# Hybrid decoder layer on one core: the output projection's two middle column blocks as seven block products each, with operand sums made under the first block and results sent by way of DRAM

## The chip, the cores and the metric

One Trainium2 chip, one of its eight cores, one launch of one program. The metric is the device time of that core in microseconds (us), smaller is better. Times are compared with the median of several runs of the kernel before; the profile is one further execution, with its own time.

## What is computed

One layer of a decoder for 512 tokens of width 2048, everything in float32. Cut to what matters here:

```python
def token_mixer(h, w_in, ..., w_o, lambda_init):
    proj = h @ w_in
    ...
    o_a = (rmsnorm(gla_chunked(...), gla_norm) * gate).reshape(B, S, GLA_V)        # 512 x 1024
    o_b = (rmsnorm(diff_attention(...), diff_norm) * (1.0 - lambda_init)).reshape(B, S, DIFF_V)   # 512 x 1024
    o = jnp.concatenate([o_a, o_b], axis=-1)
    return o @ w_o                                                                 # 512x2048 @ 2048x2048

def reference(x, ...):
    h = rmsnorm(x, attn_pre_norm[l])
    m = token_mixer(h, ...)
    x = x + rmsnorm(m, attn_post_norm[l])
    h = rmsnorm(x, ffn_pre_norm[l])
    f = conv_ffn(h, w_ffn_in[l], conv_w[l], conv_b[l], w_ffn_out[l])
    x = x + rmsnorm(f, ffn_post_norm[l])
    return x
```

The case is about `o @ w_o`, the output projection, and about what stands on either side of it.

## The kernel before, in words

**Products.** A float32 operand is split into a high part and a low part of a narrower float32 form (`act(hi, raw, AF.Copy)` on ACT, L138 or L151, then `tt(lo, raw, hi, subtract)` on DVE, L139 or L152). A product is three matmuls: high by high, high by low, low by high. The activations of all 512 tokens lie split in `ah` and `al`, 4 tiles of 128 tokens by 16 slots of 128 columns. Weights come from DRAM in granules of 512 KB into one of four buffers `raw` and are split into one of three places of `ring`. So a granule can be split when its bytes have landed and the granule three before it has been used.

**A plain column block.** `proj_n` (L198) makes 512 columns for all tokens: 8 granules, each with 24 matmuls (4 token tiles, 2 slots, 3 products) that stream 512 columns of weights past a stationary 128x128 tile of activations. That is 192 matmuls. Four PSUM banks collect the four token tiles. `step()` after each granule advances side work (`fill`, a list of generators) at a rate set in `pace`.

**A unit of seven block products.** `InUnit` (L784) makes a 512-column block with tokens and the 2048 rows of the contraction each cut in two and the columns cut in two: seven products of sums of blocks instead of eight products of blocks. Its parts are called `x0`, `z0`, `y0`, `z1`, `x1`, `y1`, `y2`. Each part has 2 granules and 48 matmuls that stream 256 columns; a unit has 336. The operand sums of the tokens' side stand in `sums`: `a11`, `a12`, `a22` are blocks of `ah`/`al` themselves, `s5` is a21-a22, `s2` is s5-a11, `s3` is s2+a12, and `s7` is a11-a21, which is written over the block a21 of `ah`/`al`. The sums of the weights' side are made by DMAs on POOL's queue that add a second block from DRAM onto a granule already loaded (`more`, L806), and by one addition on DVE (L855). All input projections but the first three blocks, and both FFN products, already run this way.

**The output projection before.** The inputs are `o_a` (slots 8 to 15, written by `turn_gate`, L927) and `o_b` (slots 0 to 7, written by `place_diff`, L934, from `dstd` in DRAM). Rows of `w_o` are taken in the order of slots 8 to 15, then 0 to 7. Three column blocks run as `proj_n` (L1039), each with `evac_m` (L1033): an ACT square with a running sum, and a DVE product with the norm's gain into `m`, in SBUF. The fourth block runs in `to_ffn` (L1044), which follows an order written out by hand on PE, ACT, DVE and POOL. For token tile t it does the block's products, `evac`, then `residual` (L1063, which needs `xr`, the layer's input, and all 2048 columns of `m`), `square`, `scale` (needs the gain row `g2`), and `turn` (PE transposes and splits into `ah`/`al` for the FFN). The four tiles are staggered so that one tile's products stand over another's norm.

**What sets the order.** Outside such hand-ordered regions a planner orders each engine's instructions, by a timeline of its own: of the instructions that it holds to be ready it takes the one that comes first in the program. Each engine then runs its list in order. `keep_in_program_order` pins an instruction behind the one written just before it on its engine. The pool `wo` (tiles `m`, `g1`, `g2`, `xr`, and spare places `xhi`/`xlo` for split weights) takes over the bytes of the mixer's pools; a tile of it waits for the last user of its own bytes.

Of the kernel before, what the change touches and what calls it, by code (L numbers as in the profile page):

```python
# [17 lines left out]
P = 128  # L18
D = 2048
S = 512  # L20
NT = S // P
KT = D // P
# [3 lines left out]
DH, DQK, DDV = 4, 128, 256  # L26
# [9 lines left out]
def hybrid_layer(ctx: ExitStack, tc: tile.TileContext, x, attn_pre_norm, w_in, w_alpha_up, b_alpha,  # L36
# [10 lines left out]
    def dma(o, i):  # L47
        return nc.sync.dma_start(out=o, in_=i)
# [3 lines left out]
    act = nc.scalar.activation  # L52
    tt = nc.vector.tensor_tensor
# [6 lines left out]
    few = ctx.enter_context(tc.tile_pool(name="few", bufs=1, side="right"))  # L60
# [19 lines left out]
    fill = []  # L80
# [3 lines left out]
    def step(n=None):  # L84
        pace[1] += pace[0]
        while pace[1] >= 1.0:
            pace[1] -= 1.0
            while fill:
                try:
                    next(fill[0])  # L90
                    break
                except StopIteration:
                    fill.pop(0)

    def drain():
        while fill:
            for _ in fill.pop(0):
                pass
# [51 lines left out]
    def split(hi, lo, src):  # L150
        act(hi, src, AF.Copy)  # L151
        tt(lo, src, hi.bitcast(F32), ALU.subtract)  # L152
# [10 lines left out]
    def bcast_row(tile_ap, row):  # L163
        dma(tile_ap, row.partition_broadcast(P))
# [178 lines left out]
    HK = KT // 2  # L343
# [16 lines left out]
    def part_of(i, j):  # L360
        return [v[:, 2 * i:2 * i + 2, HK * j:HK * (j + 1), :] for v in (ah, al)]
# [419 lines left out]
    def two(v):  # L781
        return v.rearrange("p (n x) -> p n x", n=2)

    class InUnit:  # L784
# [8 lines left out]
        def block(self, i, j, g):  # L793
            return w_in3[:, HK * i + 4 * g:HK * i + 4 * g + 4, self.cols[j]:self.cols[j] + 256]
# [136 lines left out]
            turn_block(0, j, i, u)  # L931
            turn_block(1, j, i, kept_u.pop((j, i)))

    def place_diff(i):  # L934
        for h in range(DH):
            u = qk_tile("dt")
            dma(two(u), dstd[h][:, :, 256 * i:256 * (i + 1)])
            hi, lo = (v[:, 2 * i:2 * i + 2, 2 * h:2 * h + 2, :].rearrange("p t n c -> p n t c") for v in (ah, al))
            u = u.rearrange("p (n t c) -> p n t c", n=2, t=2)
            tc.keep_in_program_order(act(hi, u, AF.Copy))  # L940
            tc.keep_in_program_order(tt(lo, u, hi.bitcast(F32), ALU.subtract))

    def gv_out(t, b):
        u = block_tile("gv")
# [77 lines left out]

    x1d = [dram.tile([P, D], F32, name=f"x1d{t}") for t in range(NT)]
# [3 lines left out]
    g1 = wp.tile([P, D], F32, name="g1")  # L1027
    g2 = wp.tile([P, D], F32, name="g2")
    bcast_row(g1, attn_post_norm[0])
    bcast_row(g2, ffn_pre_norm[0])  # L1030
    ssm = [few.tile([P, 4], F32, name=f"ssm{t}") for t in range(NT)]

    def evac_m(c, t, b):  # L1033
        sl = slice(512 * c, 512 * (c + 1))
        act(m[t][:, sl], b, AF.Square, accum_out=ssm[t][:, c:c + 1])
        tt(m[t][:, sl], b, g1[:, sl], ALU.mult)

    slots = [(s + HK) % KT for s in range(KT)]
    for c in range(3):  # L1039
        proj_n(w_o3, 512 * c, lambda t, b, c=c: evac_m(c, t, b), slots)  # L1040

    def to_ffn():  # L1044
        banks = [bank(psm) for _ in range(NT)]
        w, wa, wb, xr, rs = {}, {}, {}, {}, {}

        def weights(g):
            w[g] = granule(w_o3[:, 2 * g:2 * g + 2, 1536:2048], 2, spare=wp if g > 3 else None)

        def prods(t, *gs):
            for g in gs:
                mm_n(banks, t, g, w[g], slots)

        def evac(t):
            xr[t] = wp.tile([P, D], F32, name="xr", tag="xr", bufs=2)
            dma(xr[t], x2[t * P:(t + 1) * P, :])
            evac_m(3, t, banks[t])
            ss = small.tile([P, 1], F32, name="ss", tag="ss")
            nc.vector.reduce_sum(ss, ssm[t], axis=AX.X)  # L1060
            rs[t] = rsqrt_mean(ss, D)

        def residual(t):  # L1063
            stt(m[t], m[t], rs[t], xr[t], ALU.mult, ALU.add)
            dma(x1d[t], m[t])

        def square(t):
            ss = small.tile([P, 1], F32, name="ss", tag="ss")
            act(xr[t], m[t], AF.Square, accum_out=ss)
            rs[t] = rsqrt_mean(ss, D)  # L1070

        def scale(t):
            for i in range(4):
                sl = slice(512 * i, 512 * (i + 1))
                stt(xr[t][:, sl], m[t][:, sl], rs[t], g2[:, sl], ALU.mult, ALU.mult)
# [407 lines left out]
        nxt.z0()  # L1483

    acc = []
    ssf = [few.tile([P, 4], F32, name=f"ssf{t}") for t in range(NT)]
# [317 lines left out]
```

## Time and profile before

| what | value |
|---|---|
| median of 3 runs | 2066.2 us (2065.96 to 2068.63) |
| the profiled execution's own time | 2066.0 us |
| its span in the trace | 2064.3 us |
| granted TensorE clock | 0.999 of full speed |
| TensorE busy | 99% of the span |
| VectorE, ScalarE, GpSimd busy | 73%, 49%, 14% |
| output projection, plain blocks 1 to 3 | 594.6 to 726.5 us of the span |
| the hand-ordered region after them | from 726.5 us on |

The profile has a page of totals and views of the trace: a timeline of single instructions by engine, windows (busy time of each engine in a stretch), groups of instructions by line, and the DMA issues with their time to landing. PE is TensorE's matmuls, PEld its weight loads, DVE VectorE, ACT ScalarE, POOL GpSimd, SP the engine that issues most DMAs. A matmul's row has a start and a modelled length; consecutive matmuls overlap in the pipeline, so what one costs is the distance between two starts, not its length.

### The profile page before, as it was taken

Reading aid. Unit: us, or ns where it says so; the run is one execution under the profiler, and the core shown is the slowest. Engines: PE = TensorE matmul, PEld = TensorE weight load, DVE = VectorE, ACT = ScalarE, POOL = GpSimd, SP = SyncE. Lnnn points to the kernel's source line nnn. Section 1 sums busy time; section 2 is a strip of 40 time slices with the busy share of each in tenths; the row PEclk is TensorE's granted clock in tenths of the full one; section 3 lists DMA queues with packets and bytes.
Section 4 is the critical chain, followed back from the end, with each engine's and each line's share of the span. In section 5 each row is a group of like instructions: output and inputs, shape, how many; then the busy total and the mean of one; then the engine's idle time right before and its main releaser. Section 6 shows DMA issues by size and latency. Waiting matters only on the chain.

```text
span 2064.3 us, 35589 instructions
## 1 busy us (share of the span) xinstructions
PE 2049.0 (99%) x14453; PEld 1897.7 (92%) x14453; DVE 1510.0 (73%) x1802; ACT 1002.9 (49%) x1309; POOL 292.3 (14%) x303
## 2 busy tenths in 40 slices
PE   9999999999999999999999999999999999999998
PEld 7799999999998889899999999999999988888886
DVE  7957777666762265977777777777777888988977
ACT  5544444555552243454554454555455654444443
POOL 2012223222200000011011111111111111111100
PEclk9999999999999999999999999999999999999999
DMA  5488887888874354368577577567668796776663
GB/s 206 141 183 182 200 189 176 194 180 209 190 233 148 101 179 159 102 129 193 144 163 188 136 165 188 136 167 179 146 157 199 207 260 181 193 199 170 169 178 122
DMA packets 281611, 358.09 MB, mean 173 GB/s; under 512 B 14865, under 2 KB 223173, under 8 KB 279526
## 3 DMA queue, kind: packets, MB, share of 16 engines
q1 hardware_dynamic: 192292, 259.33, 37.4%
q0 software_dynamic: 84800, 94.38, 30.1%
q8 instruction: 113, 1.85, 0.4%
q10 hardware_dynamic: 4354, 2.10, 0.4%
q14 instruction: 52, 0.43, 0.1%
HBM read 311.20 MB, written 44.56 MB: 172 GB/s over the span
## 4 chain that ended last, share of the span: by engine, by line
PE 72%; issue 23%; POOL 2%; DVE 2%; ACT 1%; DMA 1%; POOLq 0%; DVEq 0%; ACTq 0%
PE bank L1441 6%; PE bank L1439 6%; PE bank L1440 6%; PE bank L1339 4%; PE bank L1337 4%; PE bank L1338 4%; PE bank L192 3%; PE bank L194 3%; PE bank L193 3%; PE bank L830 3%; PE bank L834 3%; PE bank L836 3%; PE bank L835 3%; PE bank L832 3%; PE bank L831 3%
## 5 line engine op out<-in xcount | busy, mean ns | idle before, releaser
L138 ACT ACTIVATE ring<-raw 128x1024 fp32r<-128x1024 f32 x315 | 333.9, 1061 | 496.5 <-PE bank L1338 109.5
L139 DVE TENSOR_TENSOR ring<-raw,ring 128x1024 fp32r<-128x1024 f32 x315 | 383.4, 1223 | 258.2 <-ACT ring L138 257.5
L138 ACT ACTIVATE ring<-rt 128x1024 fp32r<-128x1024 f32 x221 | 234.3, 1062 | 249.1 <-PE bank L1338 145.4
L1339 PE MATMUL bank<-ah,ring 128*128 128x256 f32 x1280 | 353.5, 276 | 0.8 <-DVE ring L139 0.8
L1337 PE MATMUL bank<-ah,ring 128*128 128x256 f32 x1280 | 353.5, 276 | 0.0
L1338 PE MATMUL bank<-al,ring 128*128 128x256 f32 x1280 | 353.4, 276 | 0.0
L139 DVE TENSOR_TENSOR ring<-rt,ring 128x1024 fp32r<-128x1024 f32 x221 | 270.0, 1223 | 89.8 <-ACT ring L138 86.9
L1339 PEld LDWEIGHTS bank<-ah,ring 128*128 128x128 f32 x1280 | 240.3, 188 | 1.0 <-DVE ring L139 1.0
L1337 PEld LDWEIGHTS bank<-ah,ring 128*128 128x128 f32 x1280 | 240.3, 188 | 0.1
L1338 PEld LDWEIGHTS bank<-al,ring 128*128 128x128 f32 x1280 | 240.3, 188 | 0.1
L1440 PE MATMUL bank<-ring,ah 128*128 128x512 f32 x424 | 165.0, 389 | 0.0
L1441 PE MATMUL bank<-ring,al 128*128 128x512 f32 x424 | 165.0, 389 | 0.0
L1439 PE MATMUL bank<-ring,ah 128*128 128x512 f32 x424 | 152.1, 389 | 0.0
L193 PE MATMUL bank<-ring,ah 128*128 128x512 f32 x280 | 109.3, 390 | 0.1
L192 PE MATMUL bank<-ring,ah 128*128 128x512 f32 x280 | 108.9, 393 | 0.1
L194 PE MATMUL bank<-ring,al 128*128 128x512 f32 x280 | 108.1, 390 | 0.1
L1285 POOL DMA_DIRECT2D raw<-in_w_ffn_in_dram x40 | 51.2, 1309 | 397.7 <-DVE ring L139 397.7
L1285 POOL DMA_DIRECT2D rt<-in_w_ffn_in_dram x40 | 51.0, 1288 | 324.6 <-DVE ring L139 312.9
L1441 PEld LDWEIGHTS bank<-ring,al 128*128 128x128 f32 x424 | 79.6, 188 | 16.6
L1440 PEld LDWEIGHTS bank<-ring,ah 128*128 128x128 f32 x424 | 79.6, 188 | 16.6
L1439 PEld LDWEIGHTS bank<-ring,ah 128*128 128x128 f32 x424 | 79.6, 188 | 16.5
L834 PE MATMUL bank<-ring,ah 128*128 128x256 f32 x320 | 91.8, 287 | 0.0
(393 smaller groups left out, 5671.4 us busy)
## 6 DMA issues: line engine op xcount, KB each, us to landing
raw<-in_w_ffn_in_dram SPq DMA_DIRECT2D x96, 512.0 KB, 5.0
raw<-in_w_in_dram SPq DMA_DIRECT2D x56, 512.0 KB, 4.3
raw<-in_w_ffn_out_dram SPq DMA_DIRECT2D x46, 512.0 KB, 5.8
raw<-in_w_in_dram POOLq DMA_DIRECT2D x40, 512.0 KB, 6.9
rt<-in_w_ffn_in_dram SPq DMA_DIRECT2D x40, 512.0 KB, 5.7
rt<-in_w_ffn_in_dram POOLq DMA_DIRECT2D x40, 512.0 KB, 6.2
raw<-in_w_ffn_in_dram POOLq DMA_DIRECT2D x40, 512.0 KB, 7.2
raw<-in_w_o_dram SPq DMA_DIRECT2D x32, 512.0 KB, 4.0
```

Source lines behind the costliest of these rows:

```text
L138: act(hi, raw, AF.Copy)
L139: tt(lo, raw, hi.bitcast(F32), ALU.subtract)
L192: mm(banks[t], ah[:, t, s, :], w[0][:, k, :], start=st, stop=False)
L193: mm(banks[t], ah[:, t, s, :], w[1][:, k, :], start=False, stop=False)
L194: mm(banks[t], al[:, t, s, :], w[0][:, k, :], start=False, stop=sp)
L834: mm(o, sh[:, n, kk, :], wh[:, k, :], start=st, stop=False, **NOW)
L1337: mm(o, wh, sh[:, :, kk, :], start=start and kk == 0 and n == 0, stop=False, **NOW)
L1338: mm(o, wh, sl[:, :, kk, :], start=False, stop=False, **NOW)
L1339: mm(o, wl, sh[:, :, kk, :], start=False, stop=kk == HK - 1, **NOW)
L1439: mm(b[j], sh[:, o:o + P], w[0][:, q, :], start=start and st == 0, stop=False, **NOW)
L1440: mm(b[j], sh[:, o:o + P], w[1][:, q, :], start=False, stop=False, **NOW)
L1441: mm(b[j], sl[:, o:o + P], w[0][:, q, :], start=False, stop=st == 3, **NOW)
```

## The change

Column block 0 stays a plain block. Blocks 1 and 2 become units of seven products (`OutUnit`, an `InUnit` with `w_o` as its weights). Block 3 stays in `to_ffn`. While block 0 runs, a generator `out_sums` places the heads of `o_b` in `ah`/`al` and makes `s5`, `s2` and `s3` in two passes over the four heads, one step after each granule. `s7` is split over the block a21 behind the first unit's `x0`, and a21 is loaded from `dstd` and placed again ahead of the last unit's `y2`. The units need the mixer's SBUF tiles, so the results of blocks 0 to 2 are stored to a DRAM tensor `md`, and `to_ffn` loads them (`back_m`), `xr` for the first two token tiles, and `g2` with DMAs issued by ACT between its other work.

```diff
-    def place_diff(i):
+    def load_diff(h, i, u):
+        dma(two(u), dstd[h][:, :, 256 * i:256 * (i + 1)])
+        return u
...
+    def place_diff(h, i, u):
+        hi, lo = of_head(part_of(i, 0), h)
+        u = as_block(u)
+        tc.keep_in_program_order(act(hi, u, AF.Copy))
+        tc.keep_in_program_order(tt(lo, u, hi.bitcast(F32), ALU.subtract))
...
+    def out_sums():
...
+        got = {0: fetch(0)}
         for h in range(DH):
...
+            if h + 1 < DH:
+                got[h + 1] = fetch(h + 1)
+            for i in range(2):
+                place_diff(h, i, got[h][i])
+            q = tmp("q")
+            qv = as_block(q)
+            a22 = [v.bitcast(F32) for v in of_head(part_of(1, 1), h)]
+            tt(qv, as_block(got[h][1]), a22[0], ALU.subtract)
+            tt(qv, qv, a22[1], ALU.subtract)
+            split_head("s5", h, qv)
+            got[h] += (q,)
+            yield
+        for h in range(DH):
+            d0, d1, q = (as_block(v) for v in got.pop(h))
+            a12 = [v.bitcast(F32) for v in of_head(part_of(0, 1), h)]
+            tt(q, q, d0, ALU.subtract)
+            split_head("s2", h, q)
+            tt(d0, d0, d1, ALU.subtract)
+            out_s7.append(d0)
+            tt(q, q, a12[0], ALU.add)
+            tt(q, q, a12[1], ALU.add)
+            split_head("s3", h, q)
+            yield
...
-            place_diff(0)
-            place_diff(1)
...
+    def first_out(t, b):
+        o = block_tile("mo")
+        act(o, b, AF.Square, accum_out=ssm[t][:, 0:1])
+        tt(o, b, g0, ALU.mult)
+        dma(md[t // 2][:, t % 2, 0:512], o)
...
+    def out_unit(c):
+        def done(j, i, u):
+            col = 512 * c + 256 * j
+            for n in range(2):
+                jk = row_tile("jk")
+                act(jk, two(u)[:, n, :], AF.Square, accum_out=ssm[2 * i + n][:, 2 * c + j - 1:2 * c + j])
+            tt(two(u), two(u), g12[:, None, col - 512:col - 256].to_broadcast([P, 2, 256]), ALU.mult)
+            dma(md[i][:, :, col:col + 256], two(u))
...
+    fill.append(out_sums())
+    pace[:] = 0.0, 1.0
+    step()
+    pace[:] = 1.0, 0.0
+    proj_n(w_o3, 0, first_out, slots)
+    drain()
+    outs = [out_unit(1), out_unit(2)]
+    outs[0].x0()
+    for h, r in enumerate(out_s7):
+        split(*of_head(sums["s7"], h), r)
+    outs[0].z0()
+    for i, u in enumerate(outs):
+        u.y0()
+        u.z1()
+        u.x1()
+        u.y1()
+        if i == 0:
+            outs[1].x0()
+            u.y2()
+            outs[1].z0()
+        else:
+            back = [load_diff(h, 1, qk_tile("dt")) for h in range(DH)]
+            for h in range(DH):
+                place_diff(h, 1, back[h])
+            u.y2()
     mixer.close()
...
-    for c in range(3):
-        proj_n(w_o3, 512 * c, lambda t, b, c=c: evac_m(c, t, b), slots)
...
+    def back_m(t):
+        nc.scalar.dma_start(out=m[t][:, :1536], in_=md[t // 2][:, t % 2, :])
...
+        def fetch(t):
+            xr[t] = wp.tile([P, D], F32, name="xr", tag="xr", bufs=2)
+            (nc.scalar if t < 2 else nc.sync).dma_start(out=xr[t], in_=x2[t * P:(t + 1) * P, :])
...
-        for g in (3, 5, 6, 7):
+        for g in (3, 5, 6):
             weights(g)
+        fetch(0)
+        back_m(0)
+        weights(7)
+        nc.scalar.dma_start(out=g2, in_=ffn_pre_norm[0].partition_broadcast(P))
         prods(0, 1, 2, 3, 4, 5, 6, 7)
         evac(0)
+        fetch(1)
+        back_m(1)
         residual(0)
         square(0)
         scale(0)
         prods(1, 1, 2, 3, 4, 5, 6, 7)
         evac(1)
+        back_m(2)
         turn(0, 0, 1)
         residual(1)
...
         evac(2)
+        back_m(3)
         turn(1, 0, 1)
```

More of the change, by code (lines that the diff above doesn't have):

```diff
@@ L932, in turn_gate, with of_head, as_block, fetch @@
             turn_block(1, j, i, kept_u.pop((j, i)))
-    def place_diff(i):
-        for h in range(DH):
[L936 to L941, printed above, removed]
+    def load_diff(h, i, u):
+        dma(two(u), dstd[h][:, :, 256 * i:256 * (i + 1)])
+        return u
+    def of_head(pair, h):
+        return [v[:, :, 2 * h:2 * h + 2, :].rearrange("p t n c -> p n t c") for v in pair]
+    def as_block(u):
+        return u.rearrange("p (n t c) -> p n t c", n=2, t=2)
+    def place_diff(h, i, u):
[3 more added lines that the diff above has]
+        tc.keep_in_program_order(tt(lo, u, hi.bitcast(F32), ALU.subtract))
+    out_s7 = []
+    def out_sums():
+        def fetch(h):
+            return load_diff(h, 0, qk_tile("dt")), load_diff(h, 1, block_tile("dt1"))
+        def split_head(n, h, q):
+            split(*of_head(sums[n], h), q)
+        got = {0: fetch(0)}
+        for h in range(DH):
+            if h + 1 < DH:
[21 more added lines that the diff above has]
+            yield
     def gv_out(t, b):
@@ L1017, in hybrid_layer, with block @@
             drain()
-            place_diff(0)
-            place_diff(1)
+    x1d = [dram.tile([P, D], F32, name=f"x1d{t}") for t in range(NT)]
+    md = [dram.tile([P, 2, 1536], F32, name=f"md{i}") for i in range(2)]
+    ssm = [few.tile([P, 6], F32, name=f"ssm{t}") for t in range(NT)]
+    slots = [(s + HK) % KT for s in range(KT)]
+    g0 = mx.tile([P, 512], F32, name="g0", tag="md", bufs=1)
+    g12 = mx.tile([P, 1024], F32, name="g12", tag="v", bufs=1)
+    bcast_row(g0, attn_post_norm[0, 0:512])
+    bcast_row(g12, attn_post_norm[0, 512:1536])
+    def first_out(t, b):
[3 more added lines that the diff above has]
+        dma(md[t // 2][:, t % 2, 0:512], o)
+    class OutUnit(InUnit):
+        def block(self, i, j, g):
+            k = HK * (1 - i) + 4 * g
+            return w_o3[:, k:k + 4, self.cols[j]:self.cols[j] + 256]
+    def out_unit(c):
[6 more added lines that the diff above has]
+            dma(md[i][:, :, col:col + 256], two(u))
+        return OutUnit(False, (512 * c, 512 * c + 256), done)
+    fill.append(out_sums())
[23 more added lines that the diff above has]
+            u.y2()
     mixer.close()
-    x1d = [dram.tile([P, D], F32, name=f"x1d{t}") for t in range(NT)]
     wo = ExitStack()
@@ L1026, in hybrid_layer, with evac_m @@
     m = [wp.tile([P, D], F32, name=f"m{t}") for t in range(NT)]
-    g1 = wp.tile([P, D], F32, name="g1")
+    g1 = wp.tile([P, 512], F32, name="g1")
     g2 = wp.tile([P, D], F32, name="g2")
[L1029 to L1038, printed above, removed]
-    for c in range(3):
-        proj_n(w_o3, 512 * c, lambda t, b, c=c: evac_m(c, t, b), slots)
+    bcast_row(g1, attn_post_norm[0, 1536:2048])
+    def back_m(t):
+        nc.scalar.dma_start(out=m[t][:, :1536], in_=md[t // 2][:, t % 2, :])
+    def evac_m(t, b):
+        sl = slice(1536, 2048)
+        act(m[t][:, sl], b, AF.Square, accum_out=ssm[t][:, 5:6])
+        tt(m[t][:, sl], b, g1, ALU.mult)
     def to_ffn():
@@ L1053, in prods @@
                 mm_n(banks, t, g, w[g], slots)
+        def fetch(t):
+            xr[t] = wp.tile([P, D], F32, name="xr", tag="xr", bufs=2)
+            (nc.scalar if t < 2 else nc.sync).dma_start(out=xr[t], in_=x2[t * P:(t + 1) * P, :])
         def evac(t):
[L1056 to L1058 removed]
+            if t > 1:
+                fetch(t)
+            evac_m(t, banks[t])
             ss = small.tile([P, 1], F32, name="ss", tag="ss")
@@ L1485, in hybrid_layer @@
     acc = []
-    ssf = [few.tile([P, 4], F32, name=f"ssf{t}") for t in range(NT)]
+    ssf = [v[:, :4] for v in ssm]
     downs = [down_unit(c, cb) for c in range(NG // 2) for cb in range(2)]
```

## The prediction

> **What bounds the kernel now.** I read the page of totals first, then windows over the output projection, then the timeline of single engines there.
>
> ```profile
> span 2064.3 us, 35589 instructions
> ## 1 busy us (share of the span) xinstructions
> PE 2049.0 (99%) x14453; PEld 1897.7 (92%) x14453; DVE 1510.0 (73%) x1802; ACT 1002.9 (49%) x1309; POOL 292.3 (14%) x303
> ```
>
> The profiled execution took 2066.0 us, 2064.3 of span and 1.7 around it, 0.2 under the median of 2066.2. PE is busy nearly always; whether that holds where the change is, the windows say. Columns: busy time of PE, PEld, DVE, ACT and POOL with counts, granted clock, the DMA engines' share, GB/s. Rows: blocks 0, 1, 2 and the hand-ordered region.
>
> ```profile
> 596.20:639.70 43.50, 43.50 (x199) 36.18 (x198) 19.63 (x24) 16.27 (x27) 0.00 (x0) 1.00 0.65 234
> 639.70:683.20 43.50, 43.50 (x193) 36.03 (x192) 12.47 (x13) 11.12 (x16) 0.00 (x0) 1.00 0.33 97
> 683.20:726.70 43.50, 43.50 (x193) 36.02 (x193) 12.47 (x13) 11.13 (x16) 0.00 (x0) 1.00 0.30 98
> 726.70:785.00 58.30, 58.27 (x322) 50.41 (x322) 40.48 (x49) 28.10 (x41) 7.74 (x16) 1.00 0.54 190
> ```
>
> PE never idles in the blocks; DVE works 45% of block 0 and 29% of the other two; the DMA engines are a third busy in blocks 1 and 2. So time there is the number of matmuls times their spacing, and the other engines have room. In the last row DVE is at 69%, with PE waiting on what it makes.
>
> **What is removed.** The first evacuations of blocks 0, 1 and 2 on ACT:
>
> ```profile
> 635.61 0.60 ACT L1035 ACTIVATE m<-bank 128x512 f32<-128x512 f32 x1 [0.30 <-PE bank L194]
> ...
> 679.13 0.60 ACT L1035 ACTIVATE m<-bank 128x512 f32<-128x512 f32 x1 [0.30 <-PE bank L194]
> ...
> 722.65 0.60 ACT L1035 ACTIVATE m<-bank 128x512 f32<-128x512 f32 x1 [0.30 <-PE bank L194]
> ```
>
> They are 43.52 us apart, twice: 192 matmuls at 0.2267. Two blocks go, 87.04 us.
>
> **What is added on PE.** Just before block 0 a unit of the same form runs (activations stationary, 256 columns streamed). This is its last part, 48 matmuls, and the first matmul of block 0:
>
> ```profile
> 589.06 0.36 PE L834 MATMUL bank<-ring,ah 128*128 128x256 f32 x1
> 589.25 0.28 PE L835 MATMUL bank<-ring,al 128*128 128x256 f32 x1
> ...
> 594.48 0.28 PE L836 MATMUL bank<-ring,ah 128*128 128x256 f32 x1
> 594.59 0.39 PE L192 MATMUL bank<-ring,ah 128*128 128x512 f32 x1
> ```
>
> ```profile
> L834 PEld LDWEIGHTS bank<-ring,ah 128*128 128x128 f32 x320 | 60.4, 189 | 1.2 <-issue 0.8
> ```
>
> From the second start to the last, 46 steps take 5.23 us: 0.1137 each, half of 0.2267 to within 0.4%. (The first step, 0.19, follows float32 transposes, which the new units don't have.) A part is 48 x 0.1137 = 5.46 us, a unit 38.2, two 76.4. If each part paid the 5.53 from 589.06 to 594.59, two would cost 77.4. PE saves 10.6 us, at least 9.6.
>
> Weight loads come twice as often. Their row lists 189 ns each, longer than the spacing, and still the matmuls start every 0.1137: the loads run beside the matmuls. If they didn't, a unit would cost 336 x (0.1137 + 0.189) = 101.7 and a block 192 x (0.2267 + 0.189) = 79.8, and the change would lose 43.8 us. In the Trainium skill, "TensorE: Matmul & The Clock Gate", Part 3, "The mechanism", a weight load overlaps a running matmul only when the two use different row groups; all loads here use all rows. By that rule the change would be slower; the spacing in this trace says otherwise.
>
> **What is added under block 0, at DVE.** The two placings of each head stay. New for a head are, in pass one, two subtractions and a split (its low part is on DVE), and in pass two four sums and two splits: 9 DVE instructions of 512 elements, 36 for four heads, and 12 ACT instructions.
>
> ```profile
> 603.15 1.23 DVE L139 TENSOR_TENSOR ring<-raw,ring 128x1024 fp32r<-128x1024 f32 x1 [4.12 <-ACT ring L138]
> 604.72 1.89 DVE L152 TENSOR_TENSOR al<-bank,ah 128x512 fp32r<-128x512 f32 x3 [0.34 <-ACT ah L151]
> 606.53 2.49 DVE L941 TENSOR_TENSOR al<-dt,ah 128x512 fp32r<-128x512 f32 x4
> ...
> 734.41 2.35 DVE L139 TENSOR_TENSOR xlo<-raw,xhi 128x1024 fp32r<-128x1024 f32 x2
> ```
>
> ```profile
> 639.49 0.39 PE L192 MATMUL bank<-ring,ah 128*128 128x512 f32 x1
> ```
>
> In a row such an instruction costs 0.60 (2.49 for four, the last at its full 0.69) and a granule's low part 1.13 (2.35 for two). 36 x 0.60 = 21.6 us on top of the 19.63 in block 0's window make 41.2 of 43.5: room, just. By granule: PE uses one in 24 x 0.2267 = 5.44 us, DVE needs 5 x 0.60 + 1.13 = 4.13 in pass one and 6 x 0.60 + 1.13 = 4.73 in pass two. It keeps up, but starts late: the placings are pinned behind the last turn of the gate (row 604.72), so the steps start at 606.5. Block 0 ends at 639.49, so PE wants granule 4 at 639.49 - 4 x 5.44 = 617.7. If DVE takes the steps strictly ahead of it (head 0's placings 1.2, three heads of 3.0, head 0 of pass two 3.6, the granule 1.13) it is there at 621.4, 3.7 late; if granules slip into the waits for ACT, it isn't late at all. The nearest row for a saturated DVE with such sums is the first of these windows:
>
> ```profile
> 842.00:884.00 42.00, 42.00 (x266) 37.84 (x265) 39.81 (x39) 20.12 (x23) 4.14 (x4) 1.00 0.34 77
> 614.00:626.00 12.00, 12.00 (x55) 9.94 (x54) 5.51 (x5) 4.65 (x5) 0.00 (x0) 1.00 1.00 406
> 734.00:742.00 8.00, 8.00 (x37) 6.62 (x36) 3.99 (x4) 2.50 (x4) 0.00 (x0) 1.00 0.85 271
> ```
>
> There, under the FFN's first blocks, `up_sums` fills DVE to 95%, and PE loses nothing, over the same hand-over into a first unit. I take 0.8 us of loss, between 0 and 3.7.
>
> **The first unit.** `z0` follows `x0` at once and needs weights that a DMA on POOL's queue adds.
>
> ```profile
> raw<-in_w_in_dram POOLq DMA_DIRECT2D x40, 512.0 KB, 6.9
> ```
>
> ```profile
> xr<-in_x_dram SPq DMA_DIRECT2D x4, 1024.0 KB
> ```
>
> ```profile
> 572.34 1.32 POOL L808 DMA_DIRECT2D raw<-in_w_in_dram  x1 [0.36 <-issue]
> ```
>
> The second granule of `x0` gets its place in `ring` when block 0's next to last granule is used, 5.44 us before its end T; split by T - 3.1, and issued (about 1.3), added by T + 5.1, split by T + 7.4. PE wants it at T + 5.46 + 2.73 = T + 8.2. The margin is 0.8 us, and a late DVE eats it. I take 0.3, between 0 and 3. Later parts are as in the gate's units, where PE doesn't wait. The four `s7` splits (2.4 us of DVE) and the four placings ahead of the last `y2` (2.4, due only at `to_ffn`'s third token tile) lie beside PE's 5.46 us a part. The stores to `md` go from the same five buffers as the gate units' stores.
>
> **Into the hand-ordered region.** Let E be the end of block 2: now 639.49 + 2 x 43.52 = 726.53.
>
> ```profile
> 573.44 0.52 ACTq L738 DMA_DIRECT2D dstd<-dst  x1
> ...
> 733.14 1.99 ACT L138 ACTIVATE xhi<-raw 128x1024 fp32r<-128x1024 f32 x2
> 735.94 1.06 ACT L138 ACTIVATE xhi<-raw 128x1024 fp32r<-128x1024 f32 x1 [0.81 <-DMA raw<-in_w_o_dram]
> ```
>
> ```profile
> 734.52 4.13 SPq L102 DMA_DIRECT2D raw<-in_w_ffn_in_dram  x4
> ```
>
> ```profile
> 744.11 2.35 DVE L1064 SCALAR_TENSOR_TENSOR m<-m,rs,xr 128x2048 f32<-128x2048 f32 x1 [0.94 <-POOL rs L147]
> 749.45 2.74 DVE L1075 SCALAR_TENSOR_TENSOR xr<-m,rs,g 128x512 f32<-128x512 f32 x4 [2.98 <-POOL rs L147]
> ```
>
> ```profile
> 751.02 1.94 PE L159 MATMUL bank<-ident,xr 128*128 128x128 f32 x16
> ```
>
> ```profile
> 762.54 0.70 ACT m L1035 x2
> ```
>
> ACT issues seven DMAs here, 0.52 each by the first row. Two stand ahead of the split of granule 7: it starts at 736.2 instead of 735.94 and is whole at 738.5; PE wants it at E + 5.44 + 6 x 1.36 = 740.1 (1.36 is six matmuls at 0.2267). Covered. Those ahead of `square(0)` fall into ACT's wait for `residual(0)`, but `back_m(3)` stands before tile 1's turn, in the chain of waits that starts at 762.54: 0.5 us.
>
> The new wait is `residual(0)`'s. It starts at E + 17.6 and now needs 1.75 MB (`xr`, 1024 KB; `m`, 768) issued at E + 8.6, beside the 2 MB of FFN weights that SP issues at E + 8. Behind it queue on DVE `scale(0)`, and PE's transposes at 751.02, with 0.8 us to spare (`scale(0)`'s first quarter ends at 750.2). 3.93 million bytes together take 9.7 us at the 406 GB/s of the window at 614 and 14.5 at the 271 of the window at 734: landing at E + 18.3 to E + 23.1, so PE waits between 0 and 4.7 us. Half of the weights are issued only later, so I take 0.7, by the first. `g2`, issued at about E + 11, is due at 749.45, E + 22.9; the loads for later token tiles are issued a tile, 7 x 1.36 = 9.5 us, ahead. The Trainium skill, "DMA: Bandwidth & Descriptors", "Issuing engines are not separate DMA queues", says that DMAs of all issuing engines share the same 16 DMA engines and interleave; were it otherwise, ACT's 1.84 million bytes alone would land at E + 13.1 and this 0.7 would be 0. No row here shows both queues loading at once.
>
> **Sum.** -10.6 + 0.8 + 0.3 + 0.5 + 0.7 = -8.3 on 2066.0: 2057.7, or 2057.9 beside the median.
>
> **The rivals.**
>
> *DVE starves block 0.* Granule 4 is 3.7 us late, and 1.8 more if head 0's sums don't get into DVE's free time before 603; the added weights of `z0` come 1 us late. Loss 6.5 plus 1.2 behind: 2066.2 - 10.6 + 7.7 = 2063.3, no change that shows. For it: the planner takes what comes first in the program. Against it: the window at 842. Chance 0.12.
>
> *The way back from DRAM.* Slower, at one place: `residual(0)`.
>
> ```profile
> HBM read 311.20 MB, written 44.56 MB: 172 GB/s over the span
> ```
>
> Before, `xr` and the gain rows were loaded under block 0, where DMA ran at share 1.00; now these and `m` come in the region where the share is 0.54 to 0.85. If all of `xr`, `m`, `g2` and the weights, 4.98 million bytes, had to pass ahead of it at the 172 GB/s that the whole span averages, they would land at E + 8.6 + 29 = E + 37.6, 19.2 after the spare is used: 2066.2 - 10.6 + 19.2 + 0.5 = 2075.3. It decides against the change from E + 28.5 on, where the lateness passes 10.1. Against it: `residual(0)` needs no `g2`, and the DMA engines have done 406. Chance 0.08.
>
> *The products don't get cheaper* (loads not hidden, above): 2066.2 + 43.8 = 2110. Chance 0.01.
>
> **How the numbers follow.** The forecast has 0.79: its own bounds are -10.6 with no loss (2055.6) and 2061.9, with `residual(0)`'s wait at its upper end. The range reaches up to the starved block, 2063.5, and down to 2055.3; outside it lie the slower cases and a little. About 0.2% is what a measurement of this kernel can tell from no change: 4.1 us. Faster than 2062.1: the forecast and a part of the starved cases, 0.81; the same 0.10; slower 0.09.
>
> **What would show it.** Right: the units' parts 5.46 us apart, no PE gap in them, the region's start about 10 us earlier. DVE near 95% in block 0, with PE's gaps there under 2 us in sum. `residual(0)`'s row tells which of DMA or POOL ended its wait. Wrong: a gap at block 0's granule 4, or PE idle ahead of the transposes of token tile 0 by more than 5 us; or 256-column matmuls further apart than 0.115.

## The result, and the profile after

The changed kernel takes 2061.8 us (median of 9 runs, 2058.8 to 2063.0), the kernel before 2066.4 in the same series. By the medians that is 4.6 us saved, where 8.3 were forecast; 2057.9 was expected, between 2055.3 and 2063.5. The ratio, which is of all runs of the two series and not of their medians, is 0.997, with an interval of 0.996 to 0.998: 6.2 us saved, between 4.1 and 8.3. The size of the saving is not known better than that. The profiled execution took 2060.3.

The head of its page (busy time by engine):

```profile
span 2058.6 us, 36402 instructions
## 1 busy us (share of the span) xinstructions
PE 2040.3 (99%) x14741; PEld 1904.1 (92%) x14741; DVE 1560.9 (76%) x1868; ACT 1032.4 (50%) x1365; POOL 307.4 (15%) x315
```

PE has 8.7 us less work than before, and the span is 5.7 shorter. The windows say where the rest is. (A row has the window and its length, then busy time of PE, PEld, DVE, ACT and POOL with counts, granted clock, the DMA engines' share and GB/s.) First two stages of the kernel before: from the first causal product of the attention heads to block 0, and block 0 itself.

```profile
382.35:594.59 212.24, 212.24 (x1702) 203.21 (x1701) 153.05 (x281) 121.53 (x234) 48.20 (x56) 1.00 0.86 202
594.59:639.49 44.90, 44.90 (x206) 37.32 (x205) 20.11 (x25) 17.74 (x27) 0.00 (x0) 1.00 0.64 227
```

And of the changed kernel those two, the two new units, and the start of the hand-ordered region up to the first transposes of token tile 0:

```profile
381.48:597.09 215.61, 213.05 (x1702) 203.55 (x1701) 153.35 (x282) 122.26 (x236) 48.03 (x56) 1.00 0.88 208
597.09:642.02 44.93, 44.93 (x206) 37.32 (x205) 42.85 (x63) 25.02 (x42) 2.56 (x2) 1.00 0.48 140
642.02:722.08 80.06, 79.19 (x673) 79.00 (x672) 51.43 (x52) 41.72 (x70) 12.69 (x10) 1.00 0.81 184
722.08:746.58 24.50, 24.50 (x110) 20.23 (x109) 12.64 (x14) 10.20 (x15) 1.49 (x4) 1.00 0.90 333
```

The stages compare as follows. All numbers are the spaces in us between the first matmuls of two stages, in the last row to the last matmul; "again" is a second profiled execution of the same two kernels (last of the experiments).

| stage | before | before again | changed | changed again | forecast |
|---|---|---|---|---|---|
| heads' products to block 0 | 212.24 | 213.67 | 215.61 | 215.68 | no change |
| block 0 | 44.90 | | 44.93 | 45.23 | +0.8 |
| blocks 1 and 2, or the two units | 87.04 | | 80.06 | 80.07 | 76.4 + 0.3 |
| last block to the first transposes | 24.49 | | 24.50 | 24.50 | +0.7 |
| transposes to the FFN's products | 115.14 | 115.15 | 115.12 | 115.12 | +0.5 |
| FFN's first products to its second | 746.73 | 745.30 | 745.30 | 745.30 | no change |
| the second products to the last matmul | 441.03 | 441.03 | 441.03 | 441.03 | no change |

(The kernel before again has 156.43 from block 0 to the transposes, as the first time: 751.02 - 594.59.) So the units gave 7.0 us instead of 10.6. The stage ahead of block 0, which the forecast doesn't mention, took 2.0 to 3.4 us more. Block 0, the hand-ordered region and the transposes, where 2.0 us of loss were forecast, lost 0 to 0.3. The 1.4 us more in the FFN stand only in the first of these four profiles.

In the units there are two things to see. These are PE's rows at their start, and 73 us later:

```profile
641.80 0.39 PE L194 MATMUL bank<-ring,al 128*128 128x512 f32 x1
642.03 0.28 PE L834 MATMUL bank<-ring,ah 128*128 128x256 f32 x1
642.15 0.28 PE L835 MATMUL bank<-ring,al 128*128 128x256 f32 x1
642.26 0.28 PE L836 MATMUL bank<-ring,ah 128*128 128x256 f32 x1
642.38 0.28 PE L834 MATMUL bank<-ring,ah 128*128 128x256 f32 x1
...
715.40 0.28 PE L836 MATMUL bank<-ring,ah 128*128 128x256 f32 x1
716.55 0.36 PE L834 MATMUL bank<-ring,ah 128*128 128x256 f32 x1 [0.87 <-DVE u L875]
```

The matmuls start 0.118 us apart and not 0.1137. Between 642.03 and 715.40 all 623 recorded steps do, 0.1178 in the mean. A part takes 5.65 us, and the 13 parts up to there cost 2.6 more than forecast. At 715.40 PE stops for 1.15 - 0.12 = 1.0 us, and the row names the reading of the bank by VectorE (L875, end of `y1`) as what ended that. The last part, behind the stop, runs at 0.1134.

In the stage ahead of block 0, three waits of PE, from the view of waits between 560 and 765 us:

```profile
PE bank L735 <- DVE on L728: 2.0, 1, 2.0
PE bank L834 <- DVE u L875: 0.9, 1, 0.9
PE bank L836 <- DVE ring L139: 0.5, 1, 0.5
```

The kernel before has none in that window. The first and third are in the last unit of the gate, ahead of block 0. The first is for `on`, a head's normalized tile, which is late because ACT came late to its squares. ACT's rows, of the kernel before and then of the changed one, show the store of a head's tile (L738), and behind it the squares for the next norm (L725):

```profile
570.17 0.38 ACT L737 ACTIVATE dst<-bank 128x256 f32<-128x256 f32 x1 [2.75 <-DMA dstd<-dst]
570.58 0.52 ACTq L738 DMA_DIRECT2D dstd<-dst  x1
571.23 0.38 ACT L725 ACTIVATE jk<-bank 128x256 f32<-128x256 f32 x1 [0.67 <-ACT dst L737]
```

```profile
569.82 0.39 ACT L737 ACTIVATE dst<-bank 128x256 f32<-128x256 f32 x1 [2.89 <-DMA dstd<-dst]
572.88 0.52 ACTq L738 DMA_DIRECT2D dstd<-dst  x1
573.52 0.39 ACT L725 ACTIVATE jk<-bank 128x256 f32<-128x256 f32 x1 [3.32 <-DMA ogt<-ogd]
```

Before, the store is issued 0.03 us after its data is there (570.55); now 2.67 after (570.21), and what ACT waited for is the landing of `ogt<-ogd`, a load that has nothing to do with the store. As the program is built, the loads and stores that SP and ACT issue report their landing on eight semaphores, taken in turn, and each one waits until the one that had its semaphore last has landed. The trace's semaphore records have it: in the changed kernel the store gets the semaphore of `ogt`'s load, which landed at 572.80, and ACT's wait for it ends at 572.83; in the kernel before it gets that of an earlier store, which had landed at 565.95. The second gain row (`g12`), which SP issues between `ogt`'s load and the store, makes that load the eighth one back.

### The profile page after: what moved, and what is told of

It is laid out like the page before. It is cut to its first block, busy times and chain, and to the rows that moved or that the text cites. A ratio compares the mean times of both kernels' runs of the same rounds, so it can differ in the third digit from the quotient of the medians.

```text
span 2058.6 us, 36402 instructions
## 1 busy us (share of the span) xinstructions
PE 2040.3 (99%) x14741; PEld 1904.1 (92%) x14741; DVE 1560.9 (76%) x1868; ACT 1032.4 (50%) x1365; POOL 307.4 (15%) x315
## 4 chain that ended last, share of the span: by engine, by line
PE 95%; DVE 2%; ACT 1%; issue 1%; DMA 1%; POOL 0%; DVEq 0%; POOLq 0%; ACTq 0%
PE bank L1441 12%; PE bank L1439 12%; PE bank L1440 12%; PE bank L1543 6%; PE bank L1542 6%; PE bank L1541 6%; PE bank L834 4%; PE bank L836 4%; PE bank L835 4%; PE bank L830 3%; PE bank L832 3%; PE bank L831 3%; PE bank L176 2%; PE bank L175 2%; PE bank L174 2%; PE bank L192 2%
## 5 line engine op out<-in xcount | busy, mean ns | idle before, releaser
L1542 PE MATMUL bank<-ring,ah 128*128 128x512 f32 x424 | 165.0, 389 | 0.0
L1543 PE MATMUL bank<-ring,al 128*128 128x512 f32 x424 | 165.0, 389 | 0.0
L1541 PE MATMUL bank<-ring,ah 128*128 128x512 f32 x424 | 152.1, 389 | 0.0
L834 PE MATMUL bank<-ring,ah 128*128 128x256 f32 x448 | 127.8, 285 | 0.9 <-DVE u L875 0.9
L836 PE MATMUL bank<-ring,ah 128*128 128x256 f32 x448 | 125.4, 280 | 0.5 <-DVE ring L139 0.5
L835 PE MATMUL bank<-ring,al 128*128 128x256 f32 x448 | 125.0, 279 | 0.0
L138 ACT ACTIVATE ring<-wt 128x1024 fp32r<-128x1024 f32 x60 | 63.5, 1058 | 72.5 <-PE bank L835 39.3
```

Source lines behind the costliest of these rows:

```text
L834: mm(o, sh[:, n, kk, :], wh[:, k, :], start=st, stop=False, **NOW)
L835: mm(o, sl[:, n, kk, :], wh[:, k, :], start=False, stop=False, **NOW)
L836: mm(o, sh[:, n, kk, :], wl[:, k, :], start=False, stop=sp_, **NOW)
L1541: mm(b[j], sh[:, o:o + P], w[0][:, q, :], start=start and st == 0, stop=False, **NOW)
L1542: mm(b[j], sh[:, o:o + P], w[1][:, q, :], start=False, stop=False, **NOW)
L1543: mm(b[j], sl[:, o:o + P], w[0][:, q, :], start=False, stop=st == 3, **NOW)
```

## The experiments

By time alone most edits of the changed kernel can't be told from it: its ratio to before lies between 0.996 and 0.998, and theirs overlap that. Only the late way back and the three edits together stand clear. What a single edit does is read from the rows.

**One small load more in the kernel before.**

```
+            g12 = mx.tile([P, 1024], F32, name="g12", tag="v", bufs=1)
+            bcast_row(g12[:, 0:4], attn_post_norm[0, 512:516])
             place_diff(0)
```

> The kernel before, plus one small load (4 columns of the gain row, 2 KB in all, into a tile that nothing reads) at the place where the changed kernel loads its second gain row. Theory A: the changed kernel's PE gap of 2.16 us at 574.84 comes from a count of loads: stores and loads share eight semaphores in turn, one load more makes ACT's store of the last attention head wait for the landing of a gated tile's load, and ACT's weight splits queue behind the store. Then this kernel shows the same gap and is about 2.8 us slower than before (2069). Theory B: the gap comes from the bytes of the gain rows (or from the sums under block 0): then 2 KB change nothing, 2066 within 0.1%.

Ratio to before 1.0006 (0.9998 to 1.0015): 1.2 us slower, from -0.4 to 3.1. The profile has the mechanism: the store now waits 1.6 us (data at 570.45, issue at 572.03), again for `ogt`'s load, and PE stops for 1.0 and 0.5 at 575 and 577. The stage takes 214.06.

```profile
570.06 0.39 ACT L737 ACTIVATE dst<-bank 128x256 f32<-128x256 f32 x1 [3.05 <-PE bank L735]
572.03 0.52 ACTq L738 DMA_DIRECT2D dstd<-dst  x1
```

So one load more is enough for the wait, but 2.8 us was too much for this place; by time alone it isn't settled.

**Gain rows after the gate.**

```
+    for v in (g0, g12):
+        nc.gpsimd.tensor_copy(v[:, 0:1], al[:, 2, KT - 1, 0:1].bitcast(F32))
     bcast_row(g0, attn_post_norm[0, 0:512])
```

> The changed kernel with both gain rows loaded only after the last turn of the gate (a one-column copy into each tile holds the load back), so that the loads ahead of the output projection fall on their semaphores as in the kernel before. A: the gap at 574.84 goes, block 0 starts some 2.8 us earlier, the time is about 2059.0 (2061.8 - 2.8). Rival C: the gap comes from the two new fetches of head tiles or other work ahead of block 0; then it stays and the time is 2061.8.

2059.1 us, ratio 0.9961 (0.9949 to 0.9974). The store waits no more (0.03), and the gap at 575 is gone. The stage still takes 214.23, since two other waits of PE came up: 0.6 us for the weights of `y1`, the gate unit's sixth part, and 0.9 for a gate result queued on VectorE behind the split of these weights. ACT started that split only when the weights had landed:

```profile
582.19 1.06 ACT L138 ACTIVATE ring<-raw 128x1024 fp32r<-128x1024 f32 x1 [4.26 <-DMA raw<-in_w_in_dram]
```

**The old places, without the bytes.** Both gain rows after the gate, as above, and in their old places two loads of 4 columns.

```
+    for v in (g0, g12):
+        bcast_row(v[:, 0:4], attn_post_norm[0, 0:4])
+    for v in (g0, g12):
+        nc.gpsimd.tensor_copy(v[:, 0:1], al[:, 2, KT - 1, 0:1].bitcast(F32))
```

> The changed kernel with both gain rows loaded after the gate, and in their old places two loads of 4 columns (2 KB each): the loads fall on their semaphores as in the changed kernel, without the bytes. Semaphores (A): the stage ahead of block 0 takes 215 to 219 us, as in the changed kernel, ACT's store waits for the gated tile's load, the time is 2061.8. Bytes (B): it takes 212 to 214.3, as in the kernel before and with the gain rows late, the time is about 2059.

2063.0 us, ratio 0.9974 (0.9964 to 0.9985); the stage takes 216.77, and the wait is back:

```profile
573.34 0.39 ACT L737 ACTIVATE dst<-bank 128x256 f32<-128x256 f32 x1 [2.98 <-DMA dstd<-dst]
575.70 0.52 ACTq L738 DMA_DIRECT2D dstd<-dst  x1
```

1.97 us from data to store, PE stopped for 1.4 and 0.5. For the store's wait it is the count of loads that matters, not their bytes. The intervals of this kernel and of the one above overlap, so the time alone doesn't tell them apart; the rows do.

**A different entry into the units.** The first matmul of each unit's first part is split in two of 128 columns.

```
...
-    mm(o, sh[:, n, kk, :], wh[:, k, :], start=st, stop=False, **NOW)
+    if st and seg == "x0" and self.w is w_o3:
+        mm(o[:, :P], sh[:, n, kk, :], wh[:, k, :P], start=True, stop=False, **NOW)
+        mm(o[:, P:], sh[:, n, kk, :], wh[:, k, P:], start=False, stop=False, **NOW)
+    else:
+        mm(o, sh[:, n, kk, :], wh[:, k, :], start=st, stop=False, **NOW)
...
```

> The changed kernel with only the very first matmul of each new unit's first part split in two of 128 columns: same columns, same operands, a different entry. Theory P: the 256-column matmuls have two steady spacings, 0.1133 and 0.1178 us, and which one holds is set by how PE enters the stretch; entered otherwise, it can fall to 0.1133 and save up to 14 x 0.21 = 3 us (2059), or stay by chance. Rival Q: 0.1178 comes from where the operands lie or from other engines' traffic in these units; then all 14 parts stay at 5.65 us and the time at 2061.8.

Ratio 0.9964 (0.9951 to 0.9978), 2059.9 us. PE's rows at the entry, and the window from the third matmul to the last block:

```profile
645.67 0.22 PE L836 MATMUL bank<-ring,ah 128*128 128x128 f32 x1
645.73 0.27 PE L837 MATMUL bank<-ring,ah 128*128 128x128 f32 x1
645.84 0.33 PE L840 MATMUL bank<-ring,al 128*128 128x256 f32 x1
646.01 0.28 PE L841 MATMUL bank<-ring,ah 128*128 128x256 f32 x1
646.13 0.28 PE L839 MATMUL bank<-ring,ah 128*128 128x256 f32 x1
```

```profile
645.84:723.19 77.35, 76.48 (x674) 76.31 (x674) 51.10 (x52) 41.56 (x70) 12.68 (x10) 1.00 0.83 190
```

77.5 us for both units against 80.06, with the gap at `y1` still in it: 2.5 us less. The operands, their places and the other engines' work are the same. Two short matmuls at each unit's start are the only difference, and the spacing is 0.1133 up to that gap, 70 us later.

**The same split in the fourth part of the first unit.** It is made there alone; the entries are those of the changed kernel. One execution.

```
...
-    mm(o, sh[:, n, kk, :], wh[:, k, :], start=st, stop=False, **NOW)
+    if seg == "z1" and kk == n == 0 and self.w is w_o3 and self.cols[0] < 1024:
+        mm(o[:, :P], sh[:, n, kk, :], wh[:, k, :P], start=st, stop=False, **NOW)
+        mm(o[:, P:], sh[:, n, kk, :], wh[:, k, P:], start=False, stop=False, **NOW)
+    else:
+        mm(o, sh[:, n, kk, :], wh[:, k, :], start=st, stop=False, **NOW)
...
```

> The changed kernel with one matmul split in two halves of 128 columns: the first of the first unit's fourth part (z1), with 144 matmuls of that unit ahead of it. Theory (two steady spacings, the state lasts until PE's flow is disturbed): 0.1178 in the first three parts and 0.1133 in the eleven behind it; from the units' start to the last block 3 x 5.65 + 11 x 5.46 + the gap of 1.04 = 78.1 us against 80.06. Rival (the spacing is set where PE goes over from 512 to 256 columns): it stays at 0.1178 in all parts, 80.1 us.

The units' window, cut at the split:

```profile
646.52:663.75 17.23, 17.23 (x148) 17.22 (x147) 11.31 (x11) 8.47 (x12) 4.18 (x4) 1.00 0.77 161
663.75:724.76 61.01, 60.14 (x528) 59.97 (x528) 39.95 (x41) 33.32 (x59) 8.50 (x7) 1.00 0.84 197
```

Ahead of the split (663.49, 144 matmuls in, so 16.97 / 144) the spacing is 0.1178, from there to the gap at `y1` 0.1133 (476 steps in a row). Behind that gap, in this run, it was 0.1178 again; in the changed kernel the same gap turned it to 0.1133. So in these runs a spacing lasts until PE's flow is disturbed; which of the two a disturbance leaves behind, they don't tell. The same gap at `y1` left 0.1133 behind it in five runs and 0.1178 in three. The sum is 78.24, 78.1 expected.

**`y1` by token halves.** The last unit's `y1` does all eight blocks of one pair of token tiles, then of the other, and VectorE takes the bank out in two halves.

```
+            w = [granule(None, 4, self.b22[g]) for g in range(2)]
...
+            for n in range(2):
...
+                tt(two(self.u11)[:, n, :], two(self.u11)[:, n, :], o, ALU.subtract)
```

> The changed kernel with the last unit's sixth part (y1) done token half by token half, and its result taken out of the bank in two halves. Theory: the PE gap of 1.04 us at 715.4 is the reading of the bank between y1 and y2, with nothing of another unit between them; the gap falls to under 0.2 us, the time by about 1 (2060.8); the spacing after it then stays at 0.1178 where the gap had turned it to 0.1133, which gives back 0.2. Rival: the gap comes from the four placings of the second half that are pinned there; then it stays.

A miss: 2063.4 us, ratio 0.998 (0.9971 to 0.9989). There are two gaps now:

```profile
714.17 0.28 PE L1094 MATMUL bank<-ring,ah 128*128 128x256 f32 x1
714.97 0.38 PE L1092 MATMUL bank<-ring,ah 128*128 128x256 f32 x1 [0.51 <-DVE u L1095]
...
719.05 0.50 PE L192 MATMUL bank<-ring,ah 128*128 128x512 f32 x1 [1.08 <-ACT ring L138]
```

PE waits for the reading of the first half although it is to write the other half of that bank. The second gap is for weights: `y1` holds both its places in `ring` to its end, and the next split starts late.

**`y2` in a bank of its own.**

```
+        def y2(self):
+            if self.cols[0] < 1024:
+                return InUnit.y2(self)
+            u01 = block_tile("u01")
+            act(u01, self.banks["y"], AF.Copy)
+            self.run("x0", "a22", self.t)
+            tt(u01, u01, self.banks["y"], ALU.add)
+            self.done(0, 1, u01)
```

> The changed kernel with the last unit's last part (y2) summed in a bank of its own and added to the copy of the other bank afterwards (one VectorE sum of 512 elements more at the end). If the gap of 1.04 us at 715.4 is the read-out of a bank that y2 goes on writing, it falls under 0.1 here; ScalarE's copy moves up, the region after it starts 0.8 to 1.0 us earlier. If the four placings pinned there cause it, it stays.

The gap is gone (PE busy for all of the units' window, at the slow spacing):

```profile
645.91:725.05 79.14, 79.14 (x673) 79.13 (x672) 50.05 (x51) 42.31 (x71) 12.68 (x10) 1.00 0.81 183
```

80.06 - 79.14 = 0.9 us, as expected. The four placings stand where they stood, so they have no part in the gap. The time, 2061.7 (0.9975, 0.9966 to 0.9983), can't show that much.

**More sums under block 0.** 16 more VectorE sums into a scratch tile.

```
+        more = as_block(tmp("more"))
+        got_more = of_head(part_of(1, 1), 0)[0].bitcast(F32)
...
+            for _ in range(4):
+                tt(more, got_more, a12[0], ALU.add)
```

> The changed kernel with 16 more sums of 512 elements on VectorE beside the ones under the first block (a scratch tile that nothing reads), 9 of them ahead of the first unit in VectorE's order, 7 in that unit. VectorE had 42.85 us of work in the 44.93 us of block 0; 9 x 0.60 = 5.4 more. Theory (room): the free 2.1 us take a part, the rest makes PE wait at the first unit, 2 to 4 us. Rival (starvation as forecast): granules queue behind the sums in block 0 itself and PE waits 5 us or more there. Rival (slack): the sums slip into the unit, where VectorE works 64%, and PE waits less than 0.5.

2061.7 us, 0.9976 (0.9964 to 0.9987). Block 0 and the units:

```profile
599.18:644.35 45.17, 45.10 (x206) 37.13 (x204) 44.92 (x67) 25.93 (x43) 2.23 (x2) 1.00 0.47 139
644.35:725.89 81.54, 79.32 (x672) 78.95 (x673) 59.05 (x66) 42.68 (x72) 13.03 (x11) 1.00 0.80 183
```

VectorE works 44.92 of 45.17 us, and PE still works 45.10. The price is one gap of 1.5 us in the first unit (at 655.5), between what the theories gave. PE doesn't wait for granules in block 0; the sums that don't fit slide into the unit. The first unit began at 0.1133 here, for 96 steps, and ran at 0.1178 behind that gap.

**The way back from DRAM later.** `xr` of token tile 0 is issued behind granule 7's split and `g2`, `m` behind the evacuation too.

```
-        fetch(0)
-        back_m(0)
         weights(7)
...
+        fetch(0)
         evac(0)
+        back_m(0)
```

> The changed kernel with the first token tile's xr issued 5 us later and its way back from DRAM 7.5 us later, behind the gain row. This measures the spare of residual(0), which did not wait for them in the changed kernel. If they landed just ahead of it there, at E + 17, as the forecast's rates have it (1.75 MB at 406 GB/s, with the weights beside them), residual(0) is now 6 to 8 us late and PE idles 5 to 7 us ahead of the first transposes; if they had landed within 4 us of being issued, at E + 12, it is 3 us late or less and PE idles 2 at most.

2067.7 us, ratio 1.0007 (0.9998 to 1.0016): all of the gain is gone. In this kernel, residual(0) on VectorE and the issue of `m` that it waits for:

```profile
746.41 2.35 DVE L1158 SCALAR_TENSOR_TENSOR m<-m,rs,xr 128x2048 f32<-128x2048 f32 x1 [7.53 <-DMA m<-md]
```

```profile
737.47 0.34 ACTq L1127 DMA_DIRECT2D m<-md  x1
```

In the changed kernel:

```profile
739.71 2.35 DVE L1158 SCALAR_TENSOR_TENSOR m<-m,rs,xr 128x2048 f32<-128x2048 f32 x1 [0.96 <-POOL rs L147]
```

```profile
730.24 0.38 ACTq L1127 DMA_DIRECT2D m<-md  x1
```

`m` was used 8.9 us after its issue. Counted from the last block's start (722.22 here, 722.08 there) it was issued 7.1 us later, and residual(0) came 6.6 later. PE's wait at the transposes follows from that:

```profile
PE bank L159 <- DVE xr L1169: 5.7, 1, 5.7
```

In the changed kernel the semaphore records show the landings themselves: `xr` at 735.86, and `m` at 738.44, 8.2 us after its issue and 1.3 ahead of its use. There POOL's result ended the wait, as the row says.

**All three edits** of above: gain rows after the gate, the split entry, `y2` in its own bank.

> The changed kernel with three edits at once: gain rows loaded after the gate, the first matmul of a unit's first part in two halves, the last part in its own bank. If the three are independent: units at 77.4 us less the gap, i.e. 76.5 from their start to the last block's (80.06 in the changed kernel), and the time 2061.8 - 2.7 - 2.7 - 0.9 = 2055.5, if the late gain rows bring what they did alone; 2058 if that part was only chance of the loads ahead of block 0. If the spacing of 0.1133 was chance of one entry, the units stay at 79 and the time at 2058.

2055.4 us, ratio 0.9945 (0.9933 to 0.9958), clear of the changed kernel's 0.996 to 0.998. The stages as above:

```profile
381.89:593.99 212.10, 212.10 (x1702) 203.18 (x1701) 152.05 (x280) 120.69 (x235) 48.15 (x56) 1.00 0.88 207
593.99:639.02 45.03, 45.03 (x208) 37.48 (x207) 43.86 (x65) 26.17 (x43) 3.74 (x4) 1.00 0.54 161
639.02:715.39 76.37, 76.37 (x676) 76.37 (x675) 49.91 (x52) 42.08 (x71) 12.68 (x10) 1.00 0.83 189
715.39:739.89 24.50, 24.50 (x110) 20.24 (x109) 14.22 (x15) 9.75 (x14) 1.49 (x4) 1.00 0.92 346
```

The units take the 76.4 us that the forecast had (76.5 with the two short matmuls, which lie in the window before), PE never stops from 381.89 to 739.89, and the stage ahead of block 0 is where it was before the change (212.10 against 212.24). The two waits that came up with the gain rows late are missing here, with the same loads; the weights of `y1` landed at 580.2 here and at 582.1 there.

**Both kernels once more**, without an edit.

> The kernel before, once more, for the scatter of the stage ahead of block 0 (from the first causal product of the attention heads, at 382, to block 0), which took 212.24 us before, 214.06 with one small load more, and 215.6 in the changed kernel. If the loads' semaphores cause the difference, it takes 212 to 213 again. If it is chance of DMA, anywhere from 212 to 217.

> The changed kernel once more, for the same scatter: 215 to 217.5 by the semaphores (five kernels with the same loads took 215.4 to 217.6), 212 to 217 by chance. Its units take 80.0 to 80.1 us from their start to the last block, if the state of 0.1178 is entered every time.

One execution each, 2065.7 and 2060.7 us. The stage takes 213.67 and 215.68; the units 80.07. With the others, four profiled executions whose loads fall on the semaphores as before have 212.10, 212.24, 213.67 and 214.23, and nine with the changed count 215.43 to 218.96 (four of the nine include a wait of 0.5 us at 540 us that the others lack). The two groups don't overlap; the kernel before with one small load, 214.06, lies at the edge of the first. The store ahead of the squares waited 0.03 us in each of the four, and 0.3 to 2.7 us in each of the nine.

In the changed kernel again, though, it waited only 0.3 us, since `ogt`'s load landed 4.7 us after its issue and not 6.3. PE then stopped at 585 and 588 for late weights of `y1`, as with the gain rows late. So the stage has two bounds close together, the store and those weights. In four executions (this one, gain rows late, the different entry, more sums) the weights landed 11.0 to 11.7 us after their issue, and in the other ten after 6.6 to 8.9; why stays open. So how much of the 2.0 to 3.4 us the count of loads costs on the average isn't shown.

## Why the prediction was right, and where its sum was off

*Two blocks removed, 87.04 us.* Right; block 0 kept its 44.9.

*Units of 76.4 us, 77.4 at most.* The mechanism was right, the term was too small: 80.06. The step that failed is "A part is 48 x 0.1137 = 5.46 us". It took 0.1137 us from one part of the gate's units as the spacing of all. The kernel before shows both spacings, and the step looked at one: between 100 and 595 us, some 2320 recorded steps lie near 0.1133 and 710 near 0.1178. The upper bound of 5.53 us a part came from another cause and didn't cover it. "256-column matmuls further apart than 0.115" stood among the signs of being wrong, and came true. That is 2.6 us of the 3.7. The rest is the sentence "Later parts are as in the gate's units, where PE doesn't wait": there 16 transposes stand between `y1` and `y2` (587.2 to 589.06 before), and in the new last unit nothing does. That was 1.0 us. The split entry takes the first away, the extra bank the second, and with all three edits the units take 76.4.

*Weight loads not hidden.* Rejected rightly: the loads are 0.19 us and the matmuls start every 0.113 to 0.118. The Trainium skill, "TensorE: Matmul & The Clock Gate", Part 3, "The mechanism", says in its list of what overlaps that a load overlaps a running matmul only when their row groups differ (the paragraph ahead of that list also allows a load into a background buffer). The changed kernel's trace disagrees with the rule of the list, as that of before did; whether a background buffer is the reason, no run here shows.

*VectorE in block 0, 0.8 us, and the first unit, 0.3.* Zero in the first execution; in the second, block 0 took 0.3 more, in waits for a granule at 621. VectorE at 95% was forecast and is there (42.85 of 44.93); the recorded order puts splits between the sums, so no granule stood behind all of them. The rival of the starved block was priced at 7.7 us; even with 16 sums more on top the loss was 1.5.

*residual(0), 0.7 us.* Zero. E is the start of the last block, 722.08 here. The landing was forecast at E + 18.3 at the earliest; it came at E + 16.4 (738.44 - 722.08), 1.3 us ahead of its use at E + 17.6. It lies between that forecast, with all four weight loads ahead, and the E + 13.1 of ACT's loads alone. So the term was near, and too large. The rival was near too: 7 us more of lateness cost the whole gain.

*`back_m(3)`, 0.5 us.* Zero, 115.12 against 115.14 us.

*What was missing.* The gain rows' loads were given no price. Ahead of block 0 the profiles of the changed kernel are 2.0 to 3.4 us longer than those of the kernel before. In the first of them PE's stops behind the store's wait, which no data called for, are 2.0 and 0.5 us; in the second the late weights of `y1` bring most of its stops, 0.8 us twice.

That the time still fell into the range is in part luck. Of the 2.3 us of losses that were forecast, 0 to 0.3 came. In their place came 2.6 and 1.0 in the units and 2.0 to 3.4 ahead of block 0, none of them in the sum. 10.6 less these leaves 3.6 to 5.0 us, of which the medians' 4.6 is one reading; the ratio's 6.2 is more, and the runs don't say where the difference lies.

## What to carry to other kernels

Price every instruction that a change issues ahead of the stage it is about, even a small load: it can shift which semaphore a later store has to wait for, and whatever is in order behind that store waits too. When a spacing from a trace is multiplied by hundreds of instructions, take it from all their stretches and not from one; if two values come up, both belong in the range. And where a unit of work is reused, look at what stood between its parts in the old place and is missing in the new one.

## What the runs showed of the hardware

Matmuls of 256 columns with a weight load each have two steady spacings in these runs, 0.1133 and 0.1178 us, at a granted clock of 1.00 in both. Either holds for hundreds of matmuls (623 recorded steps in a row at 0.1178, or 476 at 0.1133), until something disturbs PE's flow. Two matmuls of 128 columns in place of one were put in six places (two in the different entry, one in the fourth part, three in all edits together); behind each of them the spacing was 0.1133. That was worth 2.5 us in the different entry. In the FFN's first products of the changed kernel, where the ring's weights are the loaded operand, 6570 of 6572 recorded steps near either value are at 0.1133. That operand alone doesn't decide it: the units of the input projection that load the weights too (L830 to L832) show both, 1325 steps near 0.1133 and 160 near 0.1178 between 100 and 595 us of the kernel before.

PE doesn't write one half of a bank while VectorE reads the other half in these programs: the split `y1` waited 0.5 us for it. Whether the chip needs that or only the program's semaphores ask for it wasn't tried.
